# A hybrid encoder layer on one core: the token sums of the seven-product scheme taken from normalised rows, and token chunks worked on in pairs 0 and 4, 1 and 5, 2 and 6, 3 and 7

## The chip, the cores and the metric

The kernel runs on one core of a Trainium2 chip, as one program. The metric is the device time of that program in microseconds (us), from its first to its last instruction and a little around them; less is better. Engines are named as the profile names them: PE is TensorE (matrix products), DVE is VectorE, ACT is ScalarE, POOL is GpSimd, and SP is the queue that issues most of the DMAs. Each engine takes its instructions in the order that the built program has, and an instruction whose input is not there holds up all that stand behind it on that engine.

## The reference, cut to what matters

One layer on 1024 tokens of width 1024, all in float32:

```python
h = rms_norm(x, g_pre)                        # rows scaled by 1/rms, times g_pre
proj = h @ w_in                               # 1024 x 12288, cut into nine parts
u_a, v_a, z_a, q_b, k_b, v_b, z_b, gate_a, gate_b = split(proj)
y_a = spatial_gating(gelu(u_a), gelu(v_a), ln_g, ln_b, w_s, b_s) * silu(z_a)
y_b = mixture_of_dilations(q_b, k_b, v_b) * silu(z_b)
m = sigmoid(gate_a + ..) * (y_a @ w_pa) + sigmoid(gate_b + ..) * (y_b @ w_pb)
return x + rms_norm(m @ w_o, g_post)
```

The change touches the start of this only: `h`, the part `v_b = h @ w_in[:, v_B]`, some preparation of the spatial weights `w_s`, `ln_b` and `b_s`, and sums of `h` that later products use.

## The kernel before

**Tiling.** Tokens are cut into eight chunks of 128 (chunk c = 4b + i: half b of the tokens, place i in it), features into blocks of 128. The normalised input is held transposed, features on the partitions: `hT[j][b]` is the quarter with feature half j and token half b, four feature blocks by 512 tokens. Each value that a product uses is split into a high part of reduced precision and a float32 remainder ("h" and "l"), so a product is three matmuls: high by high, high by low, low by high. `split` (L159, L160) makes the parts: ACT copies the high part, DVE subtracts. `operand` (L106, L108) does it for weights, the low part on POOL as a rule.

**Start stage (L201 to L324, the first 150 us).** It has four kinds of work, and the change rearranges them all.

1. `norm_tile(c)` loads rows of a chunk (`xt`, 128 x 1024), squares and sums them on ACT (L225), takes the power -1/2 on POOL (L165), scales on DVE (L229, into `xn`), transposes by PE in fours of 128 x 128 into a bank of PSUM (L234), and splits the bank into `hT`.
2. `spatial_weights(q)`, q from 0 to 3, prepares four of the 16 spatial matrices: load `wsr` (L272), transpose on PE (`wsT`, L278), copy to SBUF on ACT (`wf`, L279), split and store (L283), sum its columns by a product with ones (`wsR`, L285), copy that row on DVE (`rowsum`, L286), a product of two rows for the bias (`wsB`, L290), copy it out on ACT (`wb`, L291) and store it (`wsb_d`, L292).
3. `rows_product` (L154 to L156) makes `v_b`: two blocks of 512 columns (cb = 0 and 1) for each chunk, eight feature blocks by three matmuls. The groups are chunks (0, 1), (2, 3), (4, 5, 6, 7) for cb = 0 and (0 to 3), (4 to 7) for cb = 1. `v_out` splits a finished bank (`vh` on ACT, `vl` on DVE) and stores both.
4. `sum_tile(k)`, four times, for the later seven-product scheme: POOL adds high and low parts of a feature block of all four quarters back to float32 (L250, four times 128 x 512), DVE makes the sums t3, t2, t4, t1 of them (L256), and each sum is split. `t1`, `t2`, `t3` stay in SBUF (`R`), `t4` goes to DRAM and comes back later into a quarter that is free by then (L329).

**After it.** `seven` makes each further part of `proj` with seven products in place of eight; the steps are p1 with `r11`, p6 with `t2`, p2, p7 with `t3`, p5 with `t1`, p4 with `t4`, p3. The first such block is `gates(0)`, named g0. Its weight sums s1 and s2 lie in the two buffers of tag "ws" of the pool `wpool`; the others and its result tiles lie in the pool `proj`, which takes over the SBUF of the start stage.

**What sets the order.** The code is written in the order above, with `norm_tile` and `sum_tile` hung into `rows_product` at given feature blocks. A scheduler in the language's tile layer then fixes the order on each engine. A tile that reuses a buffer waits for the last reader of that buffer. Of the buffers that matter here: `xt` and `xn` have two each; `wsr`, `shift`, `rowsum`, `wf`, `wb` have one each, in the tags x00, x01, x10, x11 and ssum, which the sums use later.

Of the kernel before, what the change touches and what calls it, by code (L numbers as in the profile page):

```python
# [36 lines left out]
def tile_hybrid_encoder(  # L37
# [163 lines left out]
    with tc.tile_pool(name="start", bufs=1) as sp:  # L201
        xts, stored = [], []

        def load_tile(c):
            xt = sp.tile([P, D], F32, tag="xt", bufs=2, name=f"xt{c}")
            nc.sync.dma_start(xt, x_t[c])
            xts.append(xt)

        load_tile(0)
# [8 lines left out]
        def norm_tile(c, ahead=2):  # L218
            b, i = divmod(c, 4)
            for d in range(len(xts), min(c + ahead, 8)):  # L220
                load_tile(d)
# [3 lines left out]
            nc.scalar.activation(xn, xt, AF.Square, accum_out=ss[:, 0:1])  # L225
            power(ss[:, 1:2], ss[:, 0:1], 1.0 / D)
            for j in range(2):
                gs = slice(512 * j, 512 * (j + 1))
                nc.vector.scalar_tensor_tensor(xn[:, gs], xt[:, gs], ss[:, 1:2], gpre[:, gs], op0=ALU.mult,  # L229
                                               op1=ALU.mult)  # L230
                pt = bank("pv", f"xT{c}{j}")
                for k in range(4):
                    kk = 4 * j + k
                    nc.tensor.transpose(pt[:, k * P:(k + 1) * P], xn[:, kk * P:(kk + 1) * P], ident)  # L234
# [9 lines left out]
        def sum_tile(k):  # L244

            xs = {}
            for j in range(2):
                for b in range(2):
                    xs[j, b] = sp.tile([P, 512], F32, tag=f"x{j}{b}", bufs=1, name=f"x{j}{b}_{k}")
                    nc.gpsimd.tensor_tensor(xs[j, b], f32(hT[j][b][0][:, k, :]), f32(hT[j][b][1][:, k, :]), ALU.add)  # L250
            t2 = sp.tile([P, 512], F32, tag="ssum", bufs=1, name=f"t2f{k}")
            for n, s, first, second, op in (("t3", xs[1, 1], xs[1, 1], xs[0, 1], ALU.subtract),
                                            ("t2", t2, xs[1, 1], xs[0, 0], ALU.add),
                                            ("t4", xs[1, 0], xs[1, 0], t2, ALU.subtract),
                                            ("t1", xs[0, 1], xs[0, 1], xs[0, 0], ALU.subtract)):
                nc.vector.tensor_tensor(s, first, second, op)  # L256
                if n in R:
                    split(R[n][0][:, k, :], R[n][1][:, k, :], s)
                else:
                    hl = [sp.tile([P, 512], F32R, tag=f"ss{q}", bufs=1, name=f"{n}{q}{k}") for q in "hl"]  # L260
                    split(*hl, s)
                    for t, d in zip(hl, t4_d):
                        nc.sync.dma_start(d[:, k, :], f32(t))
# [4 lines left out]
        def spatial_weights(q):  # L268

            wsr, shift, rowsum, wf, wb = [sp.tile([P, 512], F32, tag=t, bufs=1, name=f"{n}{q}") for n, t in (  # L270
                ("wsr", "x00"), ("shift", "x01"), ("rowsum", "x10"), ("wf", "x11"), ("wb", "ssum"))]
# [16 lines left out]
            for g in range(4):  # L288
                gs = slice(g * P, (g + 1) * P)
                nc.tensor.matmul(pb[:, gs], shift[0:2, gs], rowsum[0:2, gs], start=True, stop=True)  # L290
# [8 lines left out]
        for k in range(0, KT, 2):  # L299
            if k == 2:  # L300
                norm_tile(1, 1)
            wv += row_pair(w_in, OFF_VB, k, "vb0", (nc.gpsimd, nc.vector) if k < 4 else (nc.gpsimd, nc.gpsimd))
            if k == 0:
                load_tile(1)
            spatial_weights(k // 2)
        for cb, cs, tags in ((0, (0, 1), "mm mm"), (0, (2, 3), "sc sc"), (0, (4, 5, 6, 7), "sc tp mm mm"),
                             (1, (0, 1, 2, 3), "sc sc sc tp"), (1, (4, 5, 6, 7), "mm mm sc sc")):
            ahead = {}
            if cb == 0 and cs[0] < 4:
                ahead = {2: lambda: norm_tile(2), 5: lambda: norm_tile(3)} if cs[0] == 0 else \  # L310
                    {2 * i: (lambda c=4 + i: norm_tile(c)) for i in range(4)}
            elif cb:
                ahead = {at: (lambda k=k: sum_tile(k)) for at, k in (((4, 0), (7, 1)) if cs[0] == 0 else ((1, 2), (4, 3)))}
                if cs[0] == 0:
                    wv = rows_block(w_in, OFF_VB + 512, "vb1")
# [813 lines left out]
```

## Time and profile before

| | |
|---|---|
| median of 3 runs | 1625.04 us (1624.30 to 1626.35) |
| the profiled execution | 1626.43 us, of which the span (first to last instruction) is 1624.6 us |
| granted PE clock, mean | 0.964 |
| busy share of the span | PE 93%, PEld 78%, DVE 64%, ACT 46%, POOL 51% |
| DMA | 235.35 MB, mean 145 GB/s |

How to read the views: the busy table counts matmuls as busy by modelled ends, so it shows where PE has nothing to do but not how fast it is. A row of the windows gives, for one stretch, the busy time of each engine and, behind "PEclk", the clock that PE was granted (1.00 is full speed). A row of the timeline gives start, duration, engine, line, operation, output and inputs, and in brackets how long the engine had been idle and what released it. A row of the waits says who waited for whom, how long in total, how often, and the longest. A row of the DMA issues ends with the median time from issue to landing.

### The profile page before, as it was taken

The page shows a single profiled execution, that of the slowest core. Times are in us where ns is not written, and L with a number is a line of the kernel's source. Part 1 is how long each engine was busy: PE and PEld are TensorE (multiplying, and loading weights), DVE is VectorE, ACT ScalarE, POOL GpSimd, SP SyncE. Part 2 cuts the span into 40 slices and gives each one's busy share as a digit, 9 for nine tenths or more (in the row PEclk, how much of TensorE's full clock was granted, in tenths as well). Part 3 has the DMA queues.
Part 4 walks back from the last instruction along what each step waited for, and adds up shares of the span by engine and source line. Part 5 has one row for each costly group of instructions (what it writes and reads, how often), then busy time and mean ns, then how long its engine had stood idle before and what let it go on. Part 6 is the DMA issues. An engine that isn't in the chain of part 4 may idle for free.

```text
span 1624.6 us, 22584 instructions
## 1 busy us (share of the span) xinstructions
PE 1510.6 (93%) x7703; PEld 1263.8 (78%) x7703; DVE 1034.8 (64%) x1794; ACT 745.6 (46%) x1443; POOL 834.4 (51%) x727
## 2 busy tenths in 40 slices
PE   8959999999999999999999999989898999987876
PEld 4747999988888888788888888777786788765654
DVE  5853544467575756757564654665757552799997
ACT  5422433333433433333354535777776653442442
POOL 3532644465554555555555544454444434866764
PEclk8979999999999999999999999999999989998987
DMA  8335433334342543525242423876656656753114
GB/s 265 132 122 205 139 107 107 105 91 139 114 140 89 153 126 97 157 89 164 73 156 77 151 84 126 239 230 198 184 176 194 205 161 220 263 179 104 52 42 140
DMA packets 229187, 235.35 MB, mean 145 GB/s; under 512 B 12968, under 2 KB 173768, under 8 KB 228816
## 3 DMA queue, kind: packets, MB, share of 16 engines
q1 hardware_dynamic: 228848, 233.36, 45.5%
q8 instruction: 60, 0.98, 0.3%
q10 hardware_dynamic: 224, 0.56, 0.1%
q14 instruction: 55, 0.45, 0.1%
HBM read 165.71 MB, written 68.16 MB: 144 GB/s over the span
## 4 chain that ended last, share of the span: by engine, by line
PE 66%; DVE 16%; ACT 6%; DMA 4%; issue 4%; POOL 2%; SPq 0%; DVEq 0%; ACTq 0%; POOLq 0%
PE pa L838 3%; PE pa L839 3%; PE pa L840 3%; PE sg L514 2%; DMA vn<-v_d 1%; ACT st L651 1%; DVE vn L503 1%; PE vb L154 1%; PE vb L156 1%; PE vb L155 1%; PE pr L725 1%; PE pc L740 1%; DVE x L256 1%; DVE out L1060 1%; ACT qrh L159 1%
## 5 line engine op out<-in xcount | busy, mean ns | idle before, releaser
L108 POOL TENSOR_TENSOR wl_pa<-wr_pa,wh_pa 128x512 fp32r<-128x512 f32 x56 | 73.1, 1313 | 87.7 <-ACT wh_pa L106 68.9
L503 DVE TENSOR_SCALAR vn<-vn,mean,rstd 128x128 f32<-128x128 f32 x128 | 60.8, 529 | 29.7 <-DMA vn<-v_d 29.1
L651 ACT ACTIVATE st<-st,own 128x256 f32<-128x256 f32 (+1 forms) x128 | 63.1, 494 | 25.8 <-DVE own L647 25.1
L106 ACT ACTIVATE wh_pa<-wr_pa 128x512 fp32r<-128x512 f32 x64 | 39.1, 626 | 36.5 <-PE pa L839 21.9
L665 POOL COPY oth<-own 32x4 f32<-32x4 f32 x128 | 25.4, 198 | 53.7 <-ACT st L651 49.4
L647 DVE CUSTOM_DVE_ANT_0 st<-sc,tb 128x256 f32<-128x256 f32 x64 | 25.5, 422 | 39.2 <-PE sc L646 30.0
L160 POOL TENSOR_TENSOR vl<-vn,vh 128x512 fp32r<-128x512 f32 x32 | 41.4, 1293 | 0.8 <-ACT vh L159 0.8
L108 POOL TENSOR_TENSOR wl_wom<-ws_wom,wh_wom 128x512 fp32r<-128x512 f32 x20 | 30.7, 1545 | 21.1 <-ACT wh_wom L106 21.1
L108 POOL TENSOR_TENSOR wl_pbm<-ws_pbm,wh_pbm 128x512 fp32r<-128x512 f32 x20 | 31.4, 1577 | 16.5 <-ACT wh_pbm L106 11.4
L160 POOL TENSOR_TENSOR qcl<-q,qch 128x512 fp32r<-128x512 f32 x16 | 24.7, 1544 | 29.2 <-ACT qch L159 29.1
L160 DVE TENSOR_TENSOR vl<-vb,vh 128x512 fp32r<-128x512 f32 x16 | 10.8, 689 | 38.2 <-ACT vh L159 34.2
L1024 POOL TENSOR_TENSOR m<-m,mb 128x512 f32<-128x512 f32 x16 | 25.3, 1578 | 15.4 <-DVE m L1023 14.2
L154 PE MATMUL vb<-wh_vb,hT00h 128*128 128x512 f32 x32 | 14.2, 444 | 18.7 <-DVE vl L160 18.7
L1049 POOL TENSOR_TENSOR out<-out,gp 128x512 f32<-128x512 f32 x15 | 23.3, 1555 | 16.0 <-ACT sq L1048 16.0
L160 DVE TENSOR_TENSOR ptla<-pa,ptha 128x512 fp32r<-128x512 f32 (+1 forms) x32 | 19.8, 619 | 17.4 <-ACT ptha L159 17.4
L740 PE MATMUL pc<-ptha,va 128*128 128x256 f32 (+1 forms) x128 | 24.4, 301 | 6.8 <-ACT ptha L159 5.9
L137 DVE TENSOR_TENSOR ws_pbm<-pb,pb 128x512 f32<-128x512 f32 x20 | 23.3, 1182 | 11.2 <-POOL wl_pbm L108 6.2
L644 PE MATMUL sc<-krh,qch 128*128 128x256 f32 (+2 forms) x80 | 24.3, 306 | 6.0 <-DVE own L647 5.6
L647 DVE CUSTOM_DVE_ANT_0 st<-sc,ta 128x256 f32<-128x256 f32 x48 | 20.0, 420 | 15.1 <-PE sc L646 7.3
L160 DVE TENSOR_TENSOR ptlb<-pb,pthb 128x512 fp32r<-128x512 f32 x32 | 21.7, 687 | 10.6 <-ACT pthb L159 10.3
L520 DVE SCALAR_TENSOR_TENSOR s<-sg,lng,s 128x256 f32<-128x256 f32 x64 | 28.0, 474 | 0.0
L518 DVE SCALAR_TENSOR_TENSOR s<-sg,lng,wsb 128x256 f32<-128x256 f32 x64 | 27.7, 474 | 0.0
(2727 smaller groups left out, 6129.3 us busy)
## 6 DMA issues: line engine op xcount, KB each, us to landing
wr_pa<-in_w_proj_a_dram SPq DMA_DIRECT2D x32, 512.0 KB, 5.0
wr_g<-in_w_in_dram SPq DMA_DIRECT2D x16, 512.0 KB, 3.6
wr_va<-in_w_in_dram SPq DMA_DIRECT2D x16, 512.0 KB, 3.8
wr_u<-in_w_in_dram SPq DMA_DIRECT2D x16, 512.0 KB, 3.6
wr_z<-in_w_in_dram SPq DMA_DIRECT2D x16, 512.0 KB, 4.3
vn<-v_d SPq DMA_DIRECT2D x32, 256.0 KB, 2.8
y_d<-s SPq DMA_DIRECT2D x32, 256.0 KB, 2.4
wr_yf<-y_d SPq DMA_DIRECT2D x16, 512.0 KB, 5.1
```

The costliest lines, as they stand in the source:

```text
L106: nc.scalar.activation(hi, src, AF.Copy)
L108: low.tensor_tensor(lo, src, f32(hi), ALU.subtract)
L154: nc.tensor.matmul(ps, lhs[k][0], rh, start=(k == 0), stop=False)
L160: low.tensor_tensor(lo, src, f32(hi), ALU.subtract)
L503: nc.vector.tensor_scalar(vn[:, c, :], vn[:, c, :], mean[:, 4 * b + c, 0:1], rstd[:, 4 * b + c:4 * b + c + 1], op0=ALU.subtract, op1=ALU.mult)
L514: nc.tensor.matmul(pg[:, 256 * c:256 * (c + 1)], w[:, 2 * cp + c, :], wst, start=(w is vh and c == 0), stop=(w is vl and c == 1), skip_gro ...
L647: nc.vector.tensor_tensor_reduce(st[:, t, :n], ps[:, t, :n], bias, -1.0, -NEG, ALU.add, ALU.min, own[:, half, idx, 0:1])
L651: nc.scalar.activation(st[:, t, :n], st[:, t, :n], AF.Exp, bias=own[:, half, idx, 0:1], scale=-1.0, accum_out=own[:, half, idx, 1:2])
L740: nc.tensor.matmul(po[b][:, cs], vs[l], pw[r_], start=(done[b] == 0), stop=(done[b] == 14), skip_group_check=True)
L838: nc.tensor.matmul(pss[m], lh[:, k, :], rh, start=(q == 0 and k == 0), stop=False)
L839: nc.tensor.matmul(pss[m], lh[:, k, :], rl, start=False, stop=False)
L840: nc.tensor.matmul(pss[m], ll[:, k, :], rh, start=False, stop=last)
```

## The change

Three things change in the start stage, and nothing else.

The sums no longer come from the transposed quarters. `sum_tile(i)` takes the normalised rows of chunks i and i + 4, which hold the same place of both token halves, makes t3 and t2 on DVE and t1 and t4 on POOL in 128 x 512 rows, and a new function `transposed` transposes each sum on PE into a bank and splits it from there, as it does for `hT`. The POOL additions of high and low parts are gone; 16 fours of transposes are new.

For that the rows must live longer: `norm_tile` scales them in place, `xt` has six buffers, the chunks are normalised and multiplied in the order 0, 4, 1, 5, 2, 6, 3, 7, the groups become (0, 4), (1, 5), (2, 6, 3, 7) and for the second block (0, 4, 1, 5), (2, 6, 3, 7), and the sums are hung into the second to fourth group.

SBUF for it is found by sharing buffers: `vh` moves into the tag "ws" of `wpool`; the squares, `shift` and t1 use "th"; `wsr`, `wb` and t2 share the one buffer of tag "sa"; `wf` and t3 share "sb"; `rowsum` and t4 share "sc".

```diff
+        ORDER = [0, 4, 1, 5, 2, 6, 3, 7]
+        def scratch(tag, name):
+            return wpool.tile([P, 512], F32, tag=tag, bufs=2, name=name) if tag == "th" else \
+                sp.tile([P, 512], F32, tag=tag, name=name)
+        def load_tile():
+            c = ORDER[len(xts)]
+            xts[c] = sp.tile([P, D], F32, tag="xt", bufs=6, name=f"xt{c}")
+            nc.sync.dma_start(xts[c], x_t[c])
...
+        def transposed(hl, i, src, name):
+            pt = bank("pv", name)
+            for k in range(4):
+                nc.tensor.transpose(pt[:, k * P:(k + 1) * P], src[:, k * P:(k + 1) * P], ident)
+            split(*[t[:, :, i * P:(i + 1) * P] for t in hl], pt.rearrange("p (k n) -> p k n", k=4))
...
         def v_out(c, cb, ps):
-            vh = sp.tile([P, 512], F32R, tag="vh", bufs=2, name=f"vh{cb}{c}")
+            vh = wpool.tile([P, 512], F32R, tag="ws", bufs=2, name=f"vh{cb}{c}")
...
-                    nc.gpsimd.tensor_tensor(xs[j, b], f32(hT[j][b][0][:, k, :]), f32(hT[j][b][1][:, k, :]), ALU.add)
...
+            x = {(j, b): xts[4 * b + i][:, 512 * j:512 * (j + 1)] for j in range(2) for b in range(2)}
+            t1, t2, t3, t4 = [scratch(t, f"{n}f{i}") for n, t in (("t1", "th"), ("t2", "sa"), ("t3", "sb"), ("t4", "sc"))]
+            for n, t, first, second, op, eng in (("t3", t3, x[1, 1], x[0, 1], ALU.subtract, nc.vector),
+                                                 ("t1", t1, x[0, 1], x[0, 0], ALU.subtract, nc.gpsimd),
+                                                 ("t2", t2, t3, x[0, 0], ALU.add, nc.vector),
+                                                 ("t4", t4, x[1, 0], t2, ALU.subtract, nc.gpsimd)):
+                eng.tensor_tensor(t, first, second, op)
                 if n in R:
-                    split(R[n][0][:, k, :], R[n][1][:, k, :], s)
+                    transposed(R[n], i, t, f"{n}T{i}")
...
         def spatial_weights(q):
-            wsr, shift, rowsum, wf, wb = [sp.tile([P, 512], F32, tag=t, bufs=1, name=f"{n}{q}") for n, t in (
-                ("wsr", "x00"), ("shift", "x01"), ("rowsum", "x10"), ("wf", "x11"), ("wb", "ssum"))]
+            wsr, shift, rowsum, wf = [scratch(t, f"{n}{q}") for n, t in (
+                ("wsr", "sa"), ("shift", "th"), ("rowsum", "sc"), ("wf", "sb"))]
...
+            wb = scratch("sa", f"wb{q}")
             nc.scalar.activation(wb, pb, AF.Copy)
...
-        for cb, cs, tags in ((0, (0, 1), "mm mm"), (0, (2, 3), "sc sc"), (0, (4, 5, 6, 7), "sc tp mm mm"),
-                             (1, (0, 1, 2, 3), "sc sc sc tp"), (1, (4, 5, 6, 7), "mm mm sc sc")):
+        for cb, cs, tags, ahead in ((0, (0, 4), "mm mm", {2: norm(1), 5: norm(5)}),
+                                    (0, (1, 5), "sc sc", {0: norm(2), 2: sums(0), 3: norm(6), 5: sums(1), 6: norm(3)}),
+                                    (0, (2, 6, 3, 7), "sc tp mm mm", {0: norm(7, 0), 5: sums(2)}),
+                                    (1, (0, 4, 1, 5), "sc sc sc tp", {3: sums(3)}),
+                                    (1, (2, 6, 3, 7), "mm mm sc sc", {})):
```

In the built program the instructions move as follows. The first place is on PE, from the end of the first group to the start of the second, before the change (vb00 are the banks of the first group, vb02 of the second, and the digit behind wsR, wsB or xT's chunk tells which q or chunk).

```order
L285 MATMUL wsR3_342<-wf3_324,col_139 1x512
L156 MATMUL vb00_0_352<-wh_vb0_7_317,hT10l_103 128x512
L154 MATMUL vb00_1_353<-wh_vb0_7_317,hT10h_102 128x512
L155 MATMUL vb00_1_353<-wl_vb0_7_319,hT10h_102 128x512
L156 MATMUL vb00_1_353<-wh_vb0_7_317,hT10l_103 128x512
L290 MATMUL wsB3_345<-rowsum3_323,shift3_322 128x128 x4
L154 MATMUL vb02_0_462<-wh_vb0_0_167,hT00h_98 128x512
```

The same place on PE with the change (vb01 is now the second group, chunks 1 and 5).

```order
L283 MATMUL wsT2_290<-ident_69,wsr2_282 128x128 x4
L290 MATMUL wsR2_302<-wf2_285,col_139 1x512
L295 MATMUL wsB2_305<-rowsum2_284,shift2_283 128x128 x4
L228 MATMUL xT10_376<-ident_69,xt1_280 128x128 x4
L228 MATMUL xT11_384<-ident_69,xt1_280 128x128 x4
L283 MATMUL wsT3_331<-ident_69,wsr3_323 128x128 x4
L228 MATMUL xT50_417<-ident_69,xt5_368 128x128 x4
L290 MATMUL wsR3_343<-wf3_326,col_139 1x512
L228 MATMUL xT51_425<-ident_69,xt5_368 128x128 x4
L228 MATMUL xT20_472<-ident_69,xt2_409 128x128 x4
L295 MATMUL wsB3_346<-rowsum3_325,shift3_324 128x128 x4
L154 MATMUL vb01_0_462<-wh_vb0_0_167,hT00h_98 128x512
```

Ahead of these stand the last product of the first group and the `wsB` of round 1. Before, all four rounds of the spatial weights were done among the products of the first group; now two of the four rounds, with the transposes of chunks 1 and 5, stand behind the first group and ahead of the second, with no product between them.

The second place is the SP queue, the loads of `wsr` and the stores of `wb` before the change, in the order in which they stand.

```order
L272 DMA wsr1_239<-in_w_spatial_dram 128x4x128
...
L292 DMA wsb_d_97<-wb0_181 128x512
L272 DMA wsr2_280<-in_w_spatial_dram 128x4x128
...
L292 DMA wsb_d_97<-wb1_243 128x512
L272 DMA wsr3_321<-in_w_spatial_dram 128x4x128
...
L292 DMA wsb_d_97<-wb2_284 128x512
```

The same queue with the change, again the loads of `wsr`, the stores of `wb` and the loads of rows.

```order
L298 DMA wsb_d_97<-wb0_205 128x512
...
L277 DMA wsr1_239<-in_w_spatial_dram 128x4x128
...
L298 DMA wsb_d_97<-wb1_267 128x512
...
L277 DMA wsr2_282<-in_w_spatial_dram 128x4x128
...
L298 DMA wsb_d_97<-wb2_310 128x512
L277 DMA wsr3_323<-in_w_spatial_dram 128x4x128
...
L298 DMA wsb_d_97<-wb3_351 128x512
L213 DMA xt3_545<-in_x_dram 128x1024
L213 DMA xt7_626<-in_x_dram 128x1024
```

Each load of `wsr` now stands behind the store of the round before it, whose source lies in the same buffer, and the loads of chunks 3 and 7 stand behind the last of these stores.

The third place is DVE around the first weight sums of g0, before the change (vl04 to vl07 come from the third group of v_b, vl10 to vl17 from the fourth and fifth).

```order
L355 TENSOR_TENSOR ws_g0s1_1162<-wr_g00_1138,wr_g01_1140 128x512
L355 TENSOR_TENSOR ws_g0s2_1164<-ws_g0s1_1162,wr_g00_1138 128x512
L160 TENSOR_TENSOR vl06_727<-vb04_2_616,vh06_726 128x512
...
L160 TENSOR_TENSOR vl17_1125<-vb14_3_959,vh17_1124 128x512
L355 TENSOR_TENSOR ws_g0s3_1204<-wr_g00_1138 128x512
```

The same place on DVE with the change.

```order
L160 TENSOR_TENSOR vl13_1179<-vb12_2_1068,vh13_1178 128x512
L160 TENSOR_TENSOR vl17_1185<-vb12_3_1069,vh17_1184 128x512
L361 TENSOR_TENSOR ws_g0s1_1222<-wr_g00_1198,wr_g01_1200 128x512
L361 TENSOR_TENSOR ws_g0s2_1224<-ws_g0s1_1222,wr_g00_1198 128x512
L361 TENSOR_TENSOR ws_g0s3_1264<-wr_g00_1198 128x512
```

The sums s1 and s2 moved from the third group to behind the last low part of the start stage, since `vh` now lies in their buffers. From g0 on, the order on every engine is as before.

More of the change, by code (lines that the diff above doesn't have):

```diff
@@ L201, in tile_hybrid_encoder @@
     with tc.tile_pool(name="start", bufs=1) as sp:
[L202 to L209, printed above, removed]
+        ORDER = [0, 4, 1, 5, 2, 6, 3, 7]
+        xts, stored = {}, []
+        def scratch(tag, name):
[5 more added lines that the diff above has]
+            nc.sync.dma_start(xts[c], x_t[c])
+        load_tile()
         gpre = sp.tile([P, D], F32, name="gpre")
@@ L242, in v_out, with sum_tile @@
                 stored.append(nc.sync.dma_start(d[c * P:(c + 1) * P, 512 * cb:512 * (cb + 1)], f32(t)))
[L244 to L256, printed above, removed]
+        def sum_tile(i):
+            x = {(j, b): xts[4 * b + i][:, 512 * j:512 * (j + 1)] for j in range(2) for b in range(2)}
[5 more added lines that the diff above has]
+                eng.tensor_tensor(t, first, second, op)
@@ L257, in sum_tile @@
                 if n in R:
-                    split(R[n][0][:, k, :], R[n][1][:, k, :], s)
+                    transposed(R[n], i, t, f"{n}T{i}")
                 else:
[L260 to L263, printed above, removed]
+                    hl = [sp.tile([P, 4, P], F32R, tag=f"ss{q}", name=f"{n}{q}{i}") for q in "hl"]
@@ L265, in tile_hybrid_encoder @@
+                    transposed(hl, 0, t, f"{n}T{i}")
+                    for t_, d in zip(hl, t4_d):
+                        stored.append(nc.sync.dma_start(d[:, :, i * P:(i + 1) * P], f32(t_)))
         col = sp.tile([P, 1], F32, name="col")
@@ L279, in spatial_weights @@
             nc.scalar.activation(wf, pt, AF.Copy)
-            hl = [sp.tile([P, 512], F32R, tag=f"ss{s}", bufs=1, name=f"wt{s}{q}") for s in "hl"]
-            split(*hl, wf)
+            hl = [sp.tile([P, 4, P], F32R, tag=f"ss{s}", name=f"wt{s}{q}") for s in "hl"]
+            split(*hl, wf.rearrange("p (g n) -> p g n", g=4))
             for s in range(2):
-                nc.sync.dma_start(ws_d[q][:, :, s, :], f32(hl[s]).rearrange("p (g n) -> p g n", g=4))
+                nc.sync.dma_start(ws_d[q][:, :, s, :], f32(hl[s]))
             pr_ = bank("sc", f"wsR{q}")
@@ L300, in tile_hybrid_encoder @@
             if k == 2:
-                norm_tile(1, 1)
+                norm_tile(4, 0)
             wv += row_pair(w_in, OFF_VB, k, "vb0", (nc.gpsimd, nc.vector) if k < 4 else (nc.gpsimd, nc.gpsimd))
             if k == 0:
-                load_tile(1)
+                load_tile()
+            if k == 4:
+                load_tile()
             spatial_weights(k // 2)
-        for cb, cs, tags in ((0, (0, 1), "mm mm"), (0, (2, 3), "sc sc"), (0, (4, 5, 6, 7), "sc tp mm mm"),
-                             (1, (0, 1, 2, 3), "sc sc sc tp"), (1, (4, 5, 6, 7), "mm mm sc sc")):
[L308 to L315, printed above, removed]
+        norm, sums = (lambda c, n=1: lambda: norm_tile(c, n)), (lambda i: lambda: sum_tile(i))
+        for cb, cs, tags, ahead in ((0, (0, 4), "mm mm", {2: norm(1), 5: norm(5)}),
[3 more added lines that the diff above has]
+                                    (1, (2, 6, 3, 7), "mm mm sc sc", {})):
+            if cb and cs[0] == 0:
+                wv = rows_block(w_in, OFF_VB + 512, "vb1")
             pss = banks(tags, f"vb{cb}{cs[0]}")
```

24 lines of the change are left out of this document (10 added, 14 removed).

## The prediction

> **What bounds the kernel now.** I read the page first, for the frame: the profiled execution took 1626.43 us, of which the span below, so 1.8 us lie around it. I make the sum against that execution; it lies 1.4 us above the median of 1625.04, and I take this off at the end.
>
> ```profile
> span 1624.6 us, 22584 instructions
> ```
>
> Then the windows of the start stage, in steps of 5 us (columns: stretch, length, busy us of PE, PEld, DVE, ACT and POOL, granted PE clock, DMA share, GB/s).
>
> ```profile
> 45.00:50.00 5.00, 4.69 (x27) 3.43 (x26) 3.52 (x8) 2.51 (x5) 0.55 (x1) 1.00 0.71 231
> ...
> 80.00:85.00 5.00, 2.31 (x10) 1.29 (x8) 3.79 (x4) 0.73 (x2) 4.31 (x3) 1.00 0.42 134
> ...
> 90.00:95.00 5.00, 0.00 (x0) 0.00 (x0) 3.81 (x4) 1.04 (x3) 4.37 (x4) 0.50 0.27 105
> ```
>
> PE works nearly without a break, except for one hole that begins at 82.3 us, with its clock down to half by 90. The waits of the first 125 us name it, and the DVE rows of the timeline show what DVE did meanwhile.
>
> ```profile
> PE vb L154 <- DVE vl L160: 18.7, 1, 18.7
> ```
>
> ```profile
> 87.66 1.75 DVE L256 TENSOR_TENSOR x<-x,t2f 128x512 f32<-128x512 f32 x1
> ...
> 92.84 1.73 DVE L256 TENSOR_TENSOR x<-x,x 128x512 f32<-128x512 f32 x1 [1.15 <-POOL x L250]
> ...
> 97.97 0.68 DVE L256 TENSOR_TENSOR x<-x,t2f 128x512 f32<-128x512 f32 x1
> ...
> 100.25 1.27 DVE L160 TENSOR_TENSOR vl<-vb,vh 128x512 fp32r<-128x512 f32 x2
> ```
>
> The fourth group of v_b wants banks that two `vl` must first free, and these stand on DVE behind all four token sums. A sum that reads SBUF takes 1.75 us while POOL adds, and 0.68 us when POOL is idle (97.97). So the stage is PE's, but for a hole made by DVE and POOL.
>
> **What goes.** The POOL additions go, and on DVE the `vl` now stand ahead of the last sums. The hole goes: -18.7 us. With it goes the slow start behind it, in the chain of waits:
>
> ```profile
> 53.35 0.44 PE xT L234 x4
> ...
> 103.91 0.43 PE vb L154
> 104.34 0.24 PE vb L155
> 104.58 0.23 PE vb L156
> ```
>
> Eight matmuls from 100.98 on took 0.43 in place of 0.23 us: -1.6 us.
>
> **What is added on PE.** 16 fours of transposes at 0.44 us are +7.0 us; one four of the rows' own transposes moves to ahead of the second group, -0.4 us (paid where PE will wait anyway). The splits of the sums now read a bank and not SBUF; the row of `hT01l` below, which does so too, has 0.69 us for it, and they wait on ACT and PE only in the second group, below. [...] In 45 to 50 us four fours stand among the products and the clock is 1.00, so I charge nothing here; a group wholly at half clock is a rival below.
>
> **What is moved: the spatial weights.** This is the dear part. `wsr` and `wb` now share one buffer, so the load of round q + 1 waits until the store of round q has landed. Rounds 2 and 3 stand on PE between the first and the second group, with nothing else to do. These are the steps of a round and the marks of the stage before, in the timeline.
>
> ```profile
> 10.32 1.08 PE L278 MATMUL wsT<-ident,wsr 128*128 128x128 f32 x4 [3.92 <-DMA wsr<-in_w_spatial_dram]
> ...
> 13.21 1.86 PE L285 MATMUL wsR<-wf,col 128*1 128x512 f32 x2
> ...
> 19.35 1.76 DVE L108 TENSOR_TENSOR wl_vb<-wr_vb,wh_vb 128x512 fp32r<-128x512 f32 x1
> ...
> 36.26 0.66 PE L278 MATMUL wsT<-ident,wsr 128*128 128x128 f32 x4
> ...
> 37.34 0.60 ACT L279 ACTIVATE wf<-wsT 128x512 f32<-128x512 f32 x1 [0.38 <-DVE shift L273]
> ...
> 39.13 1.02 PE L285 MATMUL wsR<-wf,col 128*1 128x512 f32 x2
> ...
> 40.19 0.68 DVE L286 COPY rowsum<-wsR 1x512 f32<-1x512 f32 x1 [0.45 <-PE wsR L285]
> ...
> 41.21 1.15 PE L290 MATMUL wsB<-rowsum,shift 2*128 2x128 f32 x8
> ...
> 42.29 0.50 PE L154 MATMUL vb<-wh_vb,hT00h 128*128 128x512 f32 x1
> ...
> 58.60 0.40 PE L154 MATMUL vb<-wh_vb,hT01h 128*128 128x512 f32 x1
> ```
>
> The page's DMA issues give transfers of 256 and 512 KB in quiet stretches (last column: us to landing):
>
> ```profile
> wr_u<-in_w_in_dram SPq DMA_DIRECT2D x16, 512.0 KB, 3.6
> ...
> vn<-v_d SPq DMA_DIRECT2D x32, 256.0 KB, 2.8
> y_d<-s SPq DMA_DIRECT2D x32, 256.0 KB, 2.4
> ```
>
> The second group began at 42.3 us, the third at 58.6. When will the second begin now? The low part of weight 3 comes at 21.1 (19.35 + 1.76), its split of the next rows 0.6 later; about 26 products at 0.23 stand between that and `wsT` of round 1, which thus starts at 27.7. The round takes 0.66 + 0.60 + 1.02 + 0.68 + 1.15 and 0.60 for the copy of `wb` (a copy of the same size as `wf`), with hops 5.0: its store is issued at 32.7. The store takes 2.4 (as `y_d`), the load of `wsr` 2.8 (as `vn`, which also reads pieces of 512 bytes): 37.9. PE has then waited over 5 us, so round 2 runs at half clock (`wsT` 1.08, `wsR` 1.86, `wsB` doubled to 2.3): 7.4, to 45.3. The load of round 3 lands at 50.5. But on ACT the squares of chunks 1, 5 and 2 stand behind the `wb` of round 2, and on DVE twelve operations of these chunks ahead of `rowsum` of round 3. Their groups, over the first 125 us:
>
> ```profile
> L229 DVE SCALAR_TENSOR_TENSOR xn<-xt,ss,gpre 128x512 f32<-128x512 f32 x16 | 13.6, 869 | 4.3 <-POOL ss L165 4.3
> ...
> L225 ACT ACTIVATE xn<-xt 128x1024 f32<-128x1024 f32 x8 | 8.4, 1054 | 3.4 <-DMA xt<-in_x_dram 3.4
> ...
> L165 POOL TENSOR_TENSOR ss<-ss,mhalf 128x1 f32<-128x1 f32 x8 | 4.4, 551 | 25.3 <-DVE ss L164 25.3
> ...
> L160 DVE TENSOR_TENSOR hT01l<-xT,hT01h 128x512 fp32r<-128x512 f32 x4 | 2.8, 689 | 0.2
> ...
> L164 DVE TENSOR_SCALAR ss<-ss,eps 128x1 f32<-128x1 f32 x8 | 1.6, 203 | 6.1 <-ACT xn L225 6.1
> ```
>
> A square of 1.05, two powers of 0.55 that DVE waits for with 0.2 for each of three scalings of them, five scalings at 0.87, four splits at 0.69, `rowsum` 0.68: 10.5, which makes 55.8, and `wsB` 1.15: 57.0. That is +14.7 us against 42.3. From below: landings of 2.1 (as `vb_h`), full clock and scalings at 0.75 give 52 to 53; from above, with the landings of `ws_d` and `wsr` in the crowded first 60 us, 62.
>
> ```profile
> wsr<-in_w_spatial_dram SPq DMA_DIRECT2D x4, 256.0 KB, 4.7
> ws_d<-wth SPq DMA_DIRECT2D x4, 256.0 KB, 4.0
> ...
> vb_h<-vh SPq DMA_DIRECT2D x4, 256.0 KB, 2.1
> ```
>
> I take 57, since few transfers run beside this chain.
>
> **The second group** now carries the sums of places 0 and 1. Before, it took 16.3 us, of which 48 products (11.0) and eight fours (3.5) leave 1.8 of waits. Now: half clock at its start, 1.6 (as behind the hole). The load of chunk 3 needs the buffer of chunk 0, which t4 of place 0 frees about 7 us into the group; 3.6 to land (as `wr_u`), a square of 1.05, then copy and split of t2 (0.60 + 0.69) end at 13.5, since on ACT the copy stands behind that square. PE wants the bank at 10.5: 3.0. About 27 DVE operations at 0.6 to 1.75 leave 2.7 more. 7.3 against 1.8: +5.5 us (0 to 8).
>
> **At g0**, s1 and s2 wait for the stores of `vh`.
>
> ```profile
> 147.49 0.39 PE L399 MATMUL g0p<-t2h,wh_g0p 128*128 128x512 f32 x1
> ...
> 147.73 0.32 SPq L242 DMA_DIRECT2D vb_h<-vh  x1
> ...
> 151.08 0.60 ACT L375 ACTIVATE g0u<-g0p 128x512 f32<-128x512 f32 x1 [3.38 <-DMA vb_l<-vl]
> ...
> 151.73 0.50 PE L399 MATMUL g0p<-hT10h,wh_g0p 128*128 128x512 f32 x1 [1.36 <-ACT g0u L375]
> ...
> 152.61 2.82 POOL L108 TENSOR_TENSOR wl_g0p<-ws_g0s,wh_g0p 128x512 fp32r<-128x512 f32 x2 [19.19 <-ACT wh_g0p L106]
> ```
>
> In times of before: the last `vh` store leaves at 147.73 and lands 2.1 later (as `vb_h`), s2 takes 0.69, its high part 0.60, its low part 1.4: 152.5. Step p6 did its first two products by then and needs ten more, 2.3: p2 starts at 154.8 and not at 151.7, +3.1 us. The old wait of 1.36 for g0u is covered by that. From below 0, if the stores land early; from above 4. Behind g0 the order is unchanged and PE has no hole to take the delay up, so all of it reaches the end.
>
> **The sum:** -18.7 - 1.6 + 7.0 - 0.4 + 14.7 + 5.5 + 3.1 = +9.6 us: 1636.0 for the profiled execution, 1634.6 as a median. About 0.2% (3.25 us) is what a measurement of this kernel can tell from no change.
>
> **The rivals.**
> Faster: the chain of stores and loads hardly holds PE. With the second group at 47 instead of 57 (a turn of 7.5 us in place of 12) and its waits as before, the sum is -18.7 - 1.6 + 6.6 + 4.7 + 0 + 3.1 = -5.9: 1619. For it: landings are medians of crowded stretches. Against: two turns need two stores, two loads and two bodies, 20 us even at full clock, from 32. It decides where the second group starts: below 47 at the waits I give, below 53 without them. Chance 0.17.
> The same: start at 52 and 1 us more of waits, sum -18.7 - 1.6 + 6.6 + 9.7 + 1 + 3.1 = +0.1: 1625. Chance 0.13.
> Slower than forecast: landings of 4.0 and 4.7 put the start at 62 and the end at 1640. Chance 0.10.
> Half clock in the whole second group, where twelve fours and the waits now stand among 48 products: 48 more times 0.20 is 9.6 us: 1644. The 1.00 of 45 to 50 us speaks against it. Chance 0.03. [...]
> The hole stays, because `vl` again stands behind sums: then nothing of -20.3 goes and the time is 1655. The order on DVE speaks against it. Chance 0.02.
> My forecast, 1629 to 1640: 0.55.
>
> **How the numbers follow.** Slower by over 0.2% are the forecast and the three rivals above it, 0.70; within 0.2% 0.13; faster 0.17. The range from 1619 to 1645 takes in the bounds of the start (52 to 62, and 47 for the faster rival) and of the second group's waits; it leaves out about 1 in 20 above and 1 in 10 below.
>
> **What would show it.** Right: no PE wait on `vl` near 80 us; PE idle most of 32 to 57 us, at a clock near 0.5, waiting for `wsr` and `wsB`; the first product of chunks 1 and 5 near 57; a wait on t2's split or chunk 3's load some 10 us on; start stage and g0's first three steps ending some 10 us later than before. Wrong: the second group starting before 50 us, or a sum of waits in it under 2 us. A hole elsewhere, in the fourth or fifth group, would refute my reading of the weights' loads, to which I charge nothing since they are issued by 26 us and used at 110.

## The result, and the profile after

The changed kernel takes 1635.28 us in the median of 4 runs (1632.22 to 1637.66), the kernel before 1625.69 us in 4 runs on the same chip. The ratio is 1.0059, with a 95% interval of 1.0042 to 1.0075. It is slower, by 9.6 us. The profiled execution took 1632.22 us, the fastest of the four, of which the span below; before it was 1624.6.

```profile
span 1630.4 us, 22694 instructions
```

The windows of the start stage come first, as in the prediction (columns: stretch, length, busy us of PE, PEld, DVE, ACT and POOL, granted PE clock, DMA share, GB/s).

```profile
35.00:40.00 5.00, 1.09 (x4) 0.72 (x4) 0.00 (x0) 0.60 (x1) 0.00 (x0) 0.50 0.44 133
45.00:50.00 5.00, 1.79 (x8) 1.57 (x8) 2.09 (x5) 3.64 (x8) 1.09 (x2) 0.50 0.32 107
65.00:70.00 5.00, 5.00 (x31) 4.02 (x30) 4.99 (x9) 2.56 (x5) 2.96 (x3) 1.00 0.58 177
80.00:85.00 5.00, 5.00 (x27) 4.16 (x26) 2.03 (x4) 1.83 (x3) 1.29 (x1) 1.00 0.49 181
90.00:95.00 5.00, 5.00 (x28) 4.11 (x26) 1.26 (x2) 2.23 (x4) 2.30 (x2) 1.00 0.26 79
```

From 80 to 95 us PE is now full at a clock of 1.00: the hole is gone. It has come back at another place, from 31 to 58 us, most of it with the clock at 0.50. In 65 to 70 us the fours of the sums stand among the products, PE is full and the clock is 1.00. The PE rows of the timeline name what the new hole waits for.

```profile
30.63 1.15 PE L295 MATMUL wsB<-rowsum,shift 2*128 2x128 f32 x8
38.21 1.09 PE L283 MATMUL wsT<-ident,wsr 128*128 128x128 f32 x4 [6.43 <-DMA wsr<-in_w_spatial_dram]
...
42.69 2.07 PE L295 MATMUL wsB<-rowsum,shift 2*128 2x128 f32 x8 [0.77 <-DVE rowsum L291]
48.21 1.97 PE L228 MATMUL xT<-ident,xt 128*128 128x128 f32 x8 [3.45 <-DVE xt L242]
50.44 1.09 PE L283 MATMUL wsT<-ident,wsr 128*128 128x128 f32 x4 [0.26 <-DMA wsr<-in_w_spatial_dram]
...
57.23 1.15 PE L295 MATMUL wsB<-rowsum,shift 2*128 2x128 f32 x8
58.31 0.50 PE L154 MATMUL vb<-wh_vb,hT00h 128*128 128x512 f32 x1
```

Between two rounds of the spatial weights there is one whole turn: `wsB`, the store of `wb`, the load of `wsr`, `wsT`. It takes 12 us, and PE has only the rows' own transposes beside it. The second group's first product stands at 58.31 us (before: 42.29).

The second loss lies at g0. These are PE's rows there, from the first product of p1 over p6 and p2 to the first of va0p; before, the same four marks stood at 144.77, 147.49, 151.73 and 165.51 us (the first and the last of them are the first two rows).

```profile
144.77 0.39 PE L399 MATMUL g0p<-hT00h,wh_g0p 128*128 128x512 f32 x1
165.51 0.28 PE L424 MATMUL va0p<-wh_va0p,hT00h 128*128 128x256 f32 x1
```

```profile
149.06 0.39 PE L405 MATMUL g0p<-hT00h,wh_g0p 128*128 128x512 f32 x1
...
157.74 0.79 PE L405 MATMUL g0p<-t2h,wh_g0p 128*128 128x512 f32 x1 [5.81 <-ACT wh_g0p L106]
...
163.22 0.39 PE L405 MATMUL g0p<-hT10h,wh_g0p 128*128 128x512 f32 x1
...
176.82 0.28 PE L430 MATMUL va0p<-wh_va0p,hT00h 128*128 128x256 f32 x1
```

So g0 takes 27.76 us where it took 20.74, and its products after the wait run at half speed (0.79 us in the row at 157.74). Split at the first product of each group, the two profiled executions compare as follows; the forecast stands beside them, with the 16 fours shared out by group (8, 4 and 4 in the second, third and fourth).

| part | before, us | after, us | change | forecast |
|---|---|---|---|---|
| up to the second group | 42.29 | 58.31 | +16.0 | +14.7 |
| second and third group | 38.34 | 45.19 | +6.85 | +10.35 |
| fourth group | 42.38 | 23.80 | -18.6 | -18.55 |
| fifth group | 21.76 | 21.76 | 0 | 0 |
| g0 | 20.74 | 27.76 | +7.0 | +3.1 |
| up to va0p | 165.51 | 176.82 | +11.3 | +9.6 |
| the rest of the span | 1459.1 | 1453.6 | -5.5 | 0 |

### The profile page after: what moved, and what is told of

Its sections match the earlier page's. It is cut to its first block, busy times and chain, and to the rows that moved or that the text cites. A ratio compares the mean times of both kernels' runs of the same rounds, so it can differ in the third digit from the quotient of the medians.

```text
span 1630.4 us, 22694 instructions
## 1 busy us (share of the span) xinstructions
PE 1517.9 (93%) x7767; PEld 1267.9 (78%) x7767; DVE 1014.3 (62%) x1786; ACT 745.9 (46%) x1443; POOL 821.3 (50%) x719
## 4 chain that ended last, share of the span: by engine, by line
PE 65%; DVE 14%; issue 5%; ACT 5%; DMA 4%; POOL 2%; SPq 1%; DVEq 0%; POOLq 0%; ACTq 0%
PE pa L845 2%; PE pa L844 2%; PE pa L846 2%; PE sg L520 2%; DMA vn<-v_d 1%; DVE ws_wom L137 1%; PE vb L155 1%; PE vb L154 1%; PE vb L156 1%; PE pr L731 1%; ACT st L657 1%; DVE vn L509 1%; DVE out L1066 1%; ACT qrh L159 1%; PE va2p L433 1%
## 5 line engine op out<-in xcount | busy, mean ns | idle before, releaser
L650 PE MATMUL sc<-krh,qch 128*128 128x256 f32 (+2 forms) x80 | 24.3, 306 | 5.7 <-DVE own L653 5.2
L108 POOL TENSOR_TENSOR wl_vb<-wr_vb,wh_vb 128x512 fp32r<-128x512 f32 x14 | 19.1, 1371 | 17.6 <-ACT wh_vb L106 17.6
L526 DVE SCALAR_TENSOR_TENSOR s<-sg,lng,s 128x256 f32<-128x256 f32 x64 | 27.9, 473 | 0.0
```

Source lines behind the costliest of these rows:

```text
L108: low.tensor_tensor(lo, src, f32(hi), ALU.subtract)
L526: nc.vector.scalar_tensor_tensor(sd, pg[:, 1], lng[:, g:g + 1], sd, op0=ALU.mult, op1=ALU.add)
```

## The experiments

The theory: the change removes the hole (20.3 us) and pays for it with transposes, with a chain of stores and loads that PE must wait for because `wsr` and `wb` share a buffer, and with `vh` lying in tag "ws", which g0 needs. Rivals: PE stands before the second group for the rows of chunks 1, 5 and 2 and not for the weights; g0 waits for something else than `vh`; the transposes slow the clock.

**The chain taken away.** In this run `wb` gets a buffer that is free at that time.

```diff
-            wb = scratch("sa", f"wb{q}")
+            wb = wpool.tile([P, 512], F32, tag="ws", bufs=2, name=f"wb{q}")
```

> wb of the spatial weights lies in tag ws (two buffers that nothing else uses until the first vh), so a round's load of wsr no longer waits for the store of wb before it; all else is the changed kernel. My theory: PE stands from 32 to 58 us because of this chain. Then rounds 2 and 3 run inside the first group, and the second group starts near 46 us (42.3 before, one four of transposes and the rows of chunk 5 added) instead of 58.3; with half clock gone and the waits of the second group as they are, 11 to 13 us off: 1622 to 1624, ratio to before 0.998 to 0.999. Rival A: PE stands there because DVE and ACT need that time for the rows of chunks 1, 5 and 2: the start moves by under 4 us and the time by as little, 1631 to 1635. Rival B: the start moves but the second group waits as much longer for its sums, because x3's buffer and the rows come at the same absolute times: the third group still starts at 82 to 83 us, 1633 to 1635.

Measured: 1619.53 us, ratio 0.9961 (0.9948 to 0.9974), 15.8 us less than the changed kernel and more than the 11 to 13 that I expected. Its PE rows:

```profile
35.17 1.15 PE L295 MATMUL wsB<-rowsum,shift 2*128 2x128 f32 x8
38.39 0.39 PE L154 MATMUL vb<-wh_vb,hT00h 128*128 128x512 f32 x1
...
131.72 0.39 PE L405 MATMUL g0p<-hT00h,wh_g0p 128*128 128x512 f32 x1
...
159.60 0.28 PE L430 MATMUL va0p<-wh_va0p,hT00h 128*128 128x256 f32 x1
```

All four rounds are over at 35 us, inside the first group, and the second starts at 38.39, 20 us earlier than in the changed kernel and earlier than I expected (46), since the rounds now lie among products. g0 starts 17.3 us earlier; the third group gives 2.7 of the 20 back (it takes 28.13 us in place of 25.43, and four more fours of transposes stand in it). Both rivals are out: with the chain goes the whole hole, though the rows of chunks 1, 5 and 2 are still to be done. (The third group starts at 78.07 us in the changed kernel and at 58.04 here; the 82 to 83 us of my rival B were misread.)

**The chain alone, put into the kernel before.** The same sharing, with chunks in the old order.

```diff
-            wsr, shift, rowsum, wf, wb = [... ("wf", "x11"), ("wb", "ssum"))]
+            wsr, shift, rowsum, wf = [... ("wf", "x11"))]
...
+            wb = sp.tile([P, 512], F32, tag="x00", bufs=1, name=f"wb{q}")
             nc.scalar.activation(wb, pb, AF.Copy)
```

> The kernel before with one change: wb is allocated in the tag of wsr, so the load of wsr of round q + 1 waits for the store of wb of round q, as in the changed kernel; the chunks stay in the order 0 to 7. By the order of instructions, PE has the rows of chunks 2 to 5 and 23 products of the third group (chunks 4 to 7 at weights 0 to 3) to do between the rounds, which the changed kernel lacks. Theory: the chain costs what it costs because nothing stands beside it, so here it costs much less: PE waits 2 to 7 us in sum, +2 to +7 us less what the hole at 82 us takes back: 1625 to 1631. Rival: the chain costs its 15 us wherever it stands: 1638 to 1642.

Measured: 1629.02 us, ratio 1.0023 (1.0013 to 1.0034). PE's rows in this run:

```profile
36.44 1.08 PE L234 MATMUL xT<-ident,xn 128*128 128x128 f32 x4 [1.05 <-DVE ss L164]
39.81 1.97 PE L234 MATMUL xT<-ident,xn 128*128 128x128 f32 x8 [2.28 <-DVE hT01l L160]
...
41.61 0.80 PE L154 MATMUL vb<-wh_vb,hT01h 128*128 128x512 f32 x1
...
54.63 0.60 PE L278 MATMUL wsT<-ident,wsr 128*128 128x128 f32 x4
...
58.18 1.15 PE L290 MATMUL wsB<-rowsum,shift 2*128 2x128 f32 x8
...
147.84 0.39 PE L400 MATMUL g0p<-hT00h,wh_g0p 128*128 128x512 f32 x1
```

The last round stands at 54.63 and 58.18 us, as late as in the changed kernel (50.44 and 57.23). But from 41.61 us on PE works on the third group meanwhile, and g0 starts only 3.1 us later than before. Up to g0, the same chain costs 3 us where products stand beside it and about 17 where none do (in the medians 4.7 and 15.8).

**`vh` alone, put into the kernel before.**

```diff
-            vh = sp.tile([P, 512], F32R, tag="vh", bufs=2, name=f"vh{cb}{c}")
+            vh = wpool.tile([P, 512], F32R, tag="ws", bufs=2, name=f"vh{cb}{c}")
```

> The kernel before with one change: vh lies in tag ws (two buffers, which g0's s1 and s2 also use). The forecast charged 3.1 us for it. Theory: s1 and s2 wait for the last two vh stores, p6 starts some 4 to 5 us after p1, PE's clock drops, and p1's start to the first va0p takes 24 to 26 us instead of 20.74: +3 to +5 us, 1628 to 1630 us, ratio 1.002 to 1.003. Rival A: the stores land early enough, under 1 us. Rival B: the whole excess of g0 in the changed kernel (7.0 us) is due to vh, then 27.7 us and 1632 us.

Measured: 1630.29 us, ratio 1.0031 (1.0018 to 1.0044), and p1 to va0p takes 171.57 - 144.68 = 26.89 us: 6.15 more than before. That lies between what I expected and rival B. The PE row with the wait, and the windows around it:

```profile
151.33 0.50 PE L399 MATMUL g0p<-t2h,wh_g0p 128*128 128x512 f32 x1 [3.77 <-ACT wh_g0p L106]
```

```profile
150.00:152.50 2.50, 0.80 (x2) 0.30 (x2) 2.06 (x3) 1.85 (x4) 1.14 (x1) 0.87 0.95 269
152.50:155.00 2.50, 2.12 (x5) 1.74 (x6) 0.87 (x1) 2.38 (x5) 2.50 (x3) 0.50 0.99 400
155.00:157.50 2.50, 2.50 (x7) 1.93 (x7) 1.72 (x1) 0.00 (x0) 2.50 (x3) 0.50 1.00 401
```

After a wait of 3.77 us the clock is 0.50 for over 5 us, in which some 14 products take 0.43 and not 0.23 us: 2.8 us that the forecast's 3.1 lacks. The two together are 5.9 of the 6.15.

**`vh` taken out of the changed kernel, alone and with the chain.** In the fifth group `vh` lies in tags that the sums have left.

```diff
-            vh = wpool.tile([P, 512], F32R, tag="ws", bufs=2, name=f"vh{cb}{c}")
+            vh = sp.tile([P, 512], F32R, tag="s" + "ab"[c // 4], name=f"vh{cb}{c}") if cb and c % 4 > 1 \
+                else wpool.tile([P, 512], F32R, tag="ws", bufs=2, name=f"vh{cb}{c}")
```

> vh of the fifth group lies in tags sa and sb, which the sums have left by then, and no longer in ws; all else is the changed kernel. My theory: s1 and s2 of g0 wait for vh's stores; without that p6 follows p1 and p2 starts 13 us after p1's start less the 5.8 us of waiting and the slow clock behind it: 6 to 7 us off, 1628 to 1629, ratio to before 1.002. Rival: the wait of g0 is that of the stores as a whole (before, too, the third vl's store held g0u for 3.38 us), so that PE then waits as long for g0u's bank and its clock drops all the same: under 2 us off, 1633 to 1635.

> Both edits at once: wb in ws, vh of the fifth group in sa and sb. If the chain of the weights and the vh stores are the two causes and independent, their gains add up to 17 to 20 us: 1615 to 1618, ratio to before 0.994 to 0.995, that is the gain that the removal of the hole (20.3 us) leaves after 6.6 us of transposes and some waits. Rival: the gain of one is swallowed by the other or by the load of x3 in the second group: 1622 to 1628.

Measured: 1633.64 us alone, ratio 1.0054 (1.004 to 1.0069), and 1616.5 us with the chain gone too, ratio 0.9943 (0.9931 to 0.9955), in the range that I had expected. Alone it gains 1.6 us in the median, which the intervals can't tell from nothing, and 3.3 at g0 (173.48 - 148.99 = 24.49 us in place of 27.76), half of what I expected; with the chain gone g0 takes 156.00 - 131.75 = 24.25 us. The rival was nearer: something else holds g0. PE's row in the run with both:

```profile
140.66 0.50 PE L405 MATMUL g0p<-hT10h,wh_g0p 128*128 128x512 f32 x1 [3.31 <-ACT g0u L381]
```

It waits 3.31 us for g0u, before 1.36. Behind that stand the last stores of v, and in the changed kernel's trace one of them is late. First ACT's rows, then the bandwidth of 146 to 156 us in 40 slices, then the queues of 150 to 151 us (packets, MB, share of 16 engines):

```profile
149.95 0.60 ACT L159 ACTIVATE vh<-vb 128x512 fp32r<-128x512 f32 x1 [1.46 <-DMA vb_h<-vh]
153.11 0.60 ACT L159 ACTIVATE vh<-vb 128x512 fp32r<-128x512 f32 x1 [2.56 <-DMA vb_h<-vh]
```

```profile
GB/s 0 0 0 0 0 0 0 0 0 0 139 385 352 303 377 385 344 385 434 361 352 352 377 377 230 25 25 25 25 33 25 0 0 344 385 369 377 401 377 393
```

```profile
q1 hardware_dynamic: 208, 0.36, 98.0%
q8 instruction: 1, 0.02, 6.0%
```

For 1.5 us only 25 GB/s move, about a sixteenth of the 344 to 401 in the slices behind it, where all 16 DMA engines work; this points to one engine that is late with its part, and the fourth `vh` waits 2.56 us for the store of the second. Just before, one packet of the queue "instruction" took 6.0% of 16 engines for 1 us, that is 0.96 us of one engine. The kernel before has such packets at 129.5 and 164.3 us, and none among these stores, which are issued around the start of g0 (144.77). The new theory: this packet brings the next of PE's instructions, and where it falls depends on how many PE has had. The page of before agrees with that: it counts 60 packets of this queue (q8) and, on PE, 7703 matmuls and as many weight loads, 257 of them to a packet.

**The packet moved, and the order of the last stores changed.** Both runs build on the one with both edits.

```diff
+        for _ in range(64):
+            nc.tensor.matmul(pt[:, :16], idle[:, :P], idle[:, :16], start=True, stop=True)
```

> The kernel of run e3_both with 64 matmuls of 16 columns (128 instructions on PE) behind the 14 that warm up, where PE waits for wsr anyway; the order of everything else is unchanged. In the traces of the changed kernel and of the runs with its order, one packet of kind instruction falls within 2 us of the first product of g0, one DMA engine then lags (DMA 20 to 27 GB/s instead of 350 for about 1.5 us), the store of the second vh lands after 4.0 us instead of 2.4, and the fourth vh waits 2.5 to 2.9 us; before has none there. My theory: this packet fetches PE's instructions, about every 256 of them, so 128 more move it by some 15 us; then the fourth vh waits under 1 us, PE waits for g0u about 1.4 us instead of 3.3 and keeps its clock, p1's start to the first va0p takes about 21 us instead of 24.25: 3 us off, 1613 us, ratio to before 0.992. Rival: the stores land late for another reason (the order of chunks 2, 6, 3, 7), and 24 us stay: 1616 to 1617.

```diff
-                                    (1, (2, 6, 3, 7), "mm mm sc sc", {})):
+                                    (1, (2, 3, 6, 7), "mm mm sc sc", {})):
```

> The kernel of run e3_both with the chunks of the fifth group in the order 2, 3, 6, 7, as neighbours like before, so that only the addresses and the order of the last stores change; number and order of PE's instructions are those of e3_both. Theory (instruction fetch): no change, the fourth vh waits 2.5 to 2.9 us and p1's start to the first va0p takes 24 us, 1616 to 1617 us. Rival (stores to chunks 2 and 6, 512 rows apart, are slow): the second vh's store lands in 2.4 us, p1 to va0p takes 21 us, 1613 us.

(In this run `vh` of the fifth group takes its tag by `c % 2` and not by `c // 4`, so that the two tags alternate as they did.)

Measured: with the packet moved 1612.73 us, ratio 0.9929 (0.9913 to 0.9945); with the other order 1617.89 us, ratio 0.9955 (0.9941 to 0.997), and g0 takes 156.29 - 131.87 = 24.42 us as without it. In the former the packet stands at 116.1 us (in the run with both edits alone at 132.3), and ACT and PE show:

```profile
134.49 0.60 ACT L159 ACTIVATE vh<-vb 128x512 fp32r<-128x512 f32 x1 [0.88 <-DMA vb_h<-vh]
```

```profile
139.04 0.50 PE L407 MATMUL g0p<-hT10h,wh_g0p 128*128 128x512 f32 x1 [1.38 <-ACT g0u L383]
```

The fourth `vh` waits 0.88 us, PE 1.38, and g0 takes 152.81 - 132.06 = 20.75 us, the 20.74 of before. So 64 matmuls whose result nobody reads take 3.5 us off g0: they move the packet. In the median it is 3.8 us, but the intervals of the two ratios overlap.

**The packet moved into g0 of the kernel before.** The same lines in the kernel before, with 68 in place of 64.

> The kernel before with 68 matmuls of 16 columns (136 instructions on PE) behind the 14 that warm up, where PE waits for wsr anyway; nothing else changes, nor the order of anything. Before has a packet of kind instruction at 164.3 us, 19.5 us after p1 of g0 begins. In run e8_shift 128 instructions moved such a packet by 16 us. Theory: this one moves to about p1 + 1 us, among the last four stores of v, and before then gets the wait that the changed kernel had there: the fourth vh waits 2.5 to 2.9 us, PE waits 3.3 to 3.5 us for g0u instead of 1.36 and drops its clock, p1 to the first va0p takes 24.2 to 24.5 us instead of 20.74: +3.5 us, 1628 us, ratio 1.002. Rival: before's order of chunks and its stores bear the packet, no change, 1624 to 1625.

Measured: 1629.95 us, ratio 1.003 (1.0019 to 1.0041). The packet stands at 146.2 us, and PE's row is:

```profile
153.88 0.80 PE L401 MATMUL g0p<-hT10h,wh_g0p 128*128 128x512 f32 x1 [3.92 <-ACT g0u L377]
```

The fourth `vh` waits 2.92 us, and g0 takes 169.98 - 144.36 = 25.62 us. Before, too, loses some 5 us when the packet falls among these stores. That it loses more than the run with both edits has in part to do with how long the clock stays down. These windows fit the stretch at 0.50 in each, first with both edits, then here:

```profile
141.52:144.92 3.40, 3.40 (x10) 2.64 (x9) 2.18 (x2) 1.97 (x4) 3.40 (x3) 0.50 0.99 411
152.12:158.92 6.80, 5.04 (x12) 3.98 (x13) 3.65 (x4) 3.31 (x6) 4.17 (x3) 0.50 0.92 347
```

All 13 profiles agree on the packet: in seven it falls within 2 us behind the first product of g0, and there the fourth `vh` waits 2.4 to 3.0 us; in the six others it waits 0.8 to 0.9 us. But the two causes of g0 don't add up, since PE waits once for both: neither 20.7, the packet alone 24.3 to 25.6, `vh` alone 26.9, both 27.5 to 27.9 us. In the changed kernel itself the packet adds least. The next run has no such packet there (the nearest stand at 141.5 and 183.1 us, g0 begins at 157.56) and `vh` in "ws", and its g0 still takes 27.48 us, where the changed kernel's takes 27.76:

```profile
159.96 0.60 ACT L159 ACTIVATE vh<-vb 128x512 fp32r<-128x512 f32 x1 [0.90 <-DMA vb_h<-vh]
164.34 0.50 PE L405 MATMUL g0p<-t2h,wh_g0p 128*128 128x512 f32 x1 [3.89 <-ACT wh_g0p L106]
```

Without the packet PE waits 3.89 us for p6 and not 5.81, but then all of the slow clock falls on products, while with it part of the slow clock passes in the wait (the clock drops at 155.8 us, and the wait ends at 157.7).

**The transposes doubled.** Each transpose of a sum is issued twice.

```diff
-            for k in range(4):
+            for k in range(4) if hl in hT[0] + hT[1] else (0, 0, 1, 1, 2, 2, 3, 3):
```

> Each of the 64 transposes of the sums is issued twice (the second writes the same values again), so 16 more fours on PE in the second, third and fourth group; all else is the changed kernel. My theory charges a four at 0.44 us wherever it stands: +7.0 us, 1642 us, ratio to the changed kernel 1.0043. Rival A: the eight fours of the second group go into the waits that PE has there anyway: +3 to 4 us, 1638 to 1639. [...]

Measured: 1646.44 us, ratio to the kernel before 1.0128 (1.0115 to 1.0141), 11.2 us above the changed kernel. Its profile has 8.5 of these at the start of g0 (157.56 us). PE's rows in the third group:

```profile
97.13 1.04 PE L228 MATMUL t3T<-ident,t3f 128*128 128x128 f32 x8
98.01 1.04 PE L228 MATMUL t1T<-ident,t1f 128*128 128x128 f32 x8
98.80 0.48 PE L154 MATMUL vb<-wh_vb,hT10h 128*128 128x512 f32 x1
...
100.61 1.06 PE L228 MATMUL t2T<-ident,t2f 128*128 128x128 f32 x8 [0.87 <-DVE t3l L160]
```

Two fours take 0.88 us from start to start, so 0.44 for one holds: 16 of them are 7.0 of the 8.5 us. The rest is waits for DVE that PE now runs into (3.9 us in the second and third group, 2.3 in the changed kernel). The other 2.7 us of the median I can't place: g0 is as long as without the added fours, and behind it the order is the same. So the total went past the 7.0 us that I had expected, and past rival A. The granted clock in these groups is 1.00 in every window from 60 to 160 us, so the transposes did not slow the clock.

**The two kernels a second time.** Unchanged, for the part behind g0.

> The kernel before, unchanged, for a second profile. In its first one the part from the first product of pa to the last of pc took 329.8 us, in the changed kernel 325.6, in the other runs 325.8 to 330.4, with the same instructions in the same order there. If that is scatter of executions, this profile shows another length (by a us or more) in that part, while the start stage agrees within 0.3 us (g0's first product at 144.8, va0p's at 165.5). If the changed kernel really works faster there, it shows 329 to 330 again.

> The changed kernel, unchanged, for a second profile. Scatter: the part from pa to pc takes another length than 325.6 us by a us or more, while the start stage agrees (second group at 58.3, g0 at 149.1, va0p at 176.8). Otherwise 325 to 326 again.

Measured: 1625.96 and 1632.17 us, spans 1624.2 and 1630.4. The part from the first product of pa to the last of pc took 330.8 us (first profile 329.8) and 324.6 (325.6), so each differs from its own first profile by 1.0 us, and the kernels by 4 to 6: scatter of one kernel's executions hardly explains the difference, as far as two profiles of each can tell. The order of the changed kernel doesn't either: with the chain taken away that part takes 329.1 us. And the losses lie at other places each time: against its first profile, the second of before loses 2.3 us near 1052 us and wins 2.9 back near 1180. The start stage, which I expected to agree within 0.3 us, differed by 1.4 (before) and 1.0 (after) at va0p.

## Why the prediction was right, and where it was off

The forecast was 1634.6 us, between 1619 and 1645, and slower by over 0.2%. Point by point:

- **The hole and the slow clock behind it** (-20.3): right. The fourth group went from 42.38 to 23.80 us, 18.6 less, and 20.3 less without its four added fours.
- **The fours** (+7.0): right, and at full clock. The rival in which the whole second group runs at half clock did not come: doubled fours leave the clock at 1.00.
- **The start of the second group** (57.0 us): right in cause, 1.3 us too early. The marks I worked out were within a us: `wsT` of round 2 at 37.9 (38.21), of round 3 at 50.5 (50.44). Taking the chain away brought 15.8 us.
- **The second group's waits** (+5.5): too large. The second and third group grew by 6.9 us; less 12 fours at 0.44, and with the four of rows that moved ahead (0.4), 2.0 us remain, of which 1.5 are waits (2.3 in place of 0.9). Two of my terms failed. I charged 1.6 us for half clock at the start of the second group, but the clock was back before it, while PE still did transposes and spatial products (first row). And I charged 3.0 us for chunk 3's load and its square, with t2's copy behind them on ACT. ACT does wait for that load, until 69.40 us, but behind the square stands a split of chunk 6's rows (hT01), and PE waits only 0.94 us for it. For t2's low part PE waits 0.4 us, and once 1.0 us for the low part of chunk 2's rows.

```profile
56.78:58.30 1.52, 1.52 (x13) 1.24 (x11) 0.80 (x2) 1.08 (x2) 0.00 (x0) 1.00 0.88 270
```

```profile
69.40 1.06 ACT L238 ACTIVATE sqx<-xt 128x1024 bf16<-128x1024 f32 x1 [2.11 <-DMA xt<-in_x_dram]
71.81 0.66 PE L228 MATMUL t3T<-ident,t3f 128*128 128x128 f32 x4 [0.94 <-DVE hT01l L160]
```

- **g0** (+3.1): mis-sized, 7.0 measured, and this is the step that failed. The wait for the last `vh` store was right (I had s2's high part ready at 151.1 us, and with `vh` alone in the kernel before p6 starts at 151.33), but a term was missing: after such a wait PE goes on at half clock (3.77 us of wait and over 5 us at 0.50 with `vh` alone), which I had charged behind the chain and not here, so that `vh` alone costs 6.15. A packet of instructions, which I didn't look for, falls among the last stores as well; beside `vh`'s wait it adds under 1 us, and it costs 3.5 or more only once `vh` is out of the way.
- **"All of it reaches the end"**: true up to 1010 us, where the difference is still 11.4 us (g14p begins at 1010.64 and 1022.02). From there to the end the profiles of the changed kernel win 5.6 and 6.1 us back. Its two profiles have 1453.6 and 1454.6 us from va0p on, before 1459.1 and 1460.0, and the nine others, with the same work there, 1456.5 to 1461.2 (six of them in the changed order). The jumps are of 0.5 to 2.9 us, at places that differ. These are the windows from g14p's first product to the end, before and after:

```profile
1010.64:1624.64 614.00, 532.34 (x2661) 434.25 (x2659) 434.30 (x841) 339.11 (x781) 323.58 (x336) 0.93 0.55 172
1022.02:1630.42 608.40, 527.42 (x2661) 429.19 (x2659) 434.67 (x841) 338.82 (x781) 323.92 (x336) 0.94 0.56 174
```

The same instructions keep PE busy 4.9 us less (5.5 in the second profiles), at a higher mean clock (0.94, before 0.93), while its idle time differs by 1.2 us at most among the four. In windows of 0.1 us the clock is below 1.00 for 70 us of this stretch, 48 of them with PE busy, and before for 91 and 62. So most of it is time at half clock that the changed kernel was spared there. Why it was spared stays open; the packets that fall elsewhere would be one cause, and that wasn't tried. In the medians the difference is 9.6 us against 11.3 at va0p, so less was won back than in the profiles; both profiled executions of the changed kernel (1632.22 and 1632.17 us) are faster than its median.

So the total was right partly by luck: g0 cost 3.9 us more than forecast and the chain 1.3, the second and third group 3.5 less, and the rest of the span gave something back. The sign was not luck: the chain decides it. With the chain taken away the same change is faster than before by 0.4%, with `vh` out of "ws" as well by 0.6%, and with the packet moved too by 0.7% (1612.73 us, the fastest version here).

## What to carry to other kernels

A buffer that two steps of a loop share turns its store and the next load into one chain; ask what else the waiting engine has at that place, because the same chain cost 3 us among products and 17 without. Charge a wait of PE of the size seen here (3.31 to 5.99 us at g0) with the half-clock products behind it. Before believing a difference of a few us, look for late stores next to packets of the instruction queue: here 64 matmuls that do nothing moved one packet by 16 us and took 3.5 us off g0.
